# Making the low parts of the MLP weights with accumulating DMAs instead of VectorE

## The chip, the core and the metric

The kernel runs as one program on one core of a Trainium2 chip. The metric is the device time of one execution in microseconds (us), as the median of several runs. Five engines work side by side, each in the order of its own instruction stream: TensorE (PE, with its weight loads shown as PEld), VectorE (DVE), ScalarE (ACT), GpSimd (POOL) and SyncE (SP), which here only issues DMAs. They meet through semaphores.

## The reference, cut to what matters

A backbone of two layers over 512 latent tokens and 256 context tokens, model width 1024. Each layer is an attention mixer followed by an MLP with 4096 hidden units; the part that the change touches is the MLP:

```
def sq_relu_mlp(h, w1, w2):
    return jnp.square(jax.nn.relu(h @ w1)) @ w2

x  = layer_norm(alpha * x + g_m * sq_relu_mlp(x * (1.0 + sc_m) + sh_m, mlp_w1[i], mlp_w2[i]), ...)
if need_ctx:   # only in the first layer: the context tokens go through the same MLP
    xc = layer_norm(alpha * xc + cg_m * sq_relu_mlp(xc * (1.0 + csc_m) + csh_m, mlp_w1[i], mlp_w2[i]), ...)
```

Everything is float32. So the first MLP (layer 0) has 768 tokens, in six tiles of 128, and the second (layer 1) has 512, in four.

## The kernel before

Matrix products are made in a three-term form. A float32 operand x is split into a high part, x rounded to the type fp32r, and a low part, x minus that high part, rounded to fp32r as well. A product is then high times high, high times low and low times high: three matmuls where one would stand.

A weight block is 128 rows of 1024 float32 values, 512 KB. `weight()` (line 72) brings one in: SP issues a DMA from HBM into a `raw` tile (line 69; three buffers, shared with the loads of `w_ada`), ACT writes the high part `wh` as a cast of `raw` (`split_hi`, line 62), and DVE writes the low part `wl` as `raw` minus `wh` (`split_lo`, line 65). There are six buffers of `wh` and six of `wl`. A `raw` buffer is free for the next load when DVE has read it.

`mlp()` (from line 940 on) takes the 4096 hidden units in sixteen chunks c of two blocks each (G = 2). For one chunk, `up(c)` brings in two blocks of `w1` and `up_mm(c)` multiplies them with the activations: TensorE lines 977 (wh with the activations' high part), 980 (wh with their low part) and 981 (wl with their high part), once for each of eight slices k, so the first matmul that reads `wl` is the third of its group. `up_end(c)` makes the hidden tile: ReLU on ACT (line 988), square on DVE (line 989), high part `hh` on ACT (line 62), low part `hl` on DVE (line 65). `w2_of(c)` brings in two blocks of `w2`, and `down(i, ...)` multiplies them for each token tile i with `hh` and `hl`: TensorE lines 89 (high, high), 90 (the one that reads `wl`) and 91. DVE adds the result to `yacc` (line 1059); for the first chunk ACT copies it (line 1057). The loop of a chunk is: `w2_of(c)`, `up(c+1)` with its matmuls, then `down` of chunk c. The last two chunks (R = 2) are multiplied together after the loop. In layer 1, where all tiles have one gate, the `w2` blocks of these last two chunks, four in all, are multiplied by the gate on POOL first (`gate=`, line 75).

In layer 0, steps of other work are put between the tiles of a chunk (`fill`, `ada_vec` from line 177 on): the loads of `w_ada`, weighted sums of them on DVE (line 197), on ACT (line 206) and on POOL (line 208, one pass over a 128x1024 tile).

The order in which each engine takes its instructions is not the order of the program text. The framework simulates the kernel while building it and orders each engine's stream by that simulation. Once built, a stream is fixed: an instruction whose operand is late holds up everything behind it on its engine. So TensorE can take the first matmuls of the next `up` between the tiles of a `down`, where the simulation saw the `down` waiting.

Of the kernel before, what the change touches and what calls it, by code (L numbers as in the profile page):

```python
# [11 lines left out]
F32 = mybir.dt.float32  # L12
F32R = mybir.dt.float32r
AF = mybir.ActivationFunctionType
ALU = mybir.AluOpType
# [4 lines left out]
P = 128  # L20
# [14 lines left out]
G = 2  # L35
# [4 lines left out]
def backbone(ctx, tc, a, out):  # L40
# [3 lines left out]
    nc = tc.nc  # L44
# [16 lines left out]
    def split_hi(dst, src):  # L61
        return nc.scalar.copy(out=dst, in_=src)  # L62

    def split_lo(dst, src, hi):
        return nc.vector.tensor_tensor(out=dst, in0=src, in1=hi.bitcast(F32), op=ALU.subtract)  # L65

    def raw_tile(src, n):
        raw = wpool.tile([P, 1024], F32, name="raw", tag="raw", bufs=3)
        nc.sync.dma_start(raw[:, 0:n], src)
        return raw  # L70

    def weight(src, n=1024, wp=None, tiles=None, gate=None):
        raw = raw_tile(src, n)
        if gate is not None:
            nc.gpsimd.tensor_tensor(out=raw, in0=raw, in1=gate, op=ALU.mult)
        if tiles is not None:
            wh, wl = tiles
        elif wp is None:
            wh = wpool.tile([P, 1024], F32R, name="wh", tag="wh", bufs=6)
            wl = wpool.tile([P, 1024], F32R, name="wl", tag="wl", bufs=6)  # L80
        else:
            wh = wp.tile([P, 1024], F32R, name="wxh", tag="wxh", bufs=2)
            wl = wp.tile([P, 1024], F32R, name="wxl", tag="wxl", bufs=2)
        split_hi(wh[:, 0:n], raw[:, 0:n])
        split_lo(wl[:, 0:n], raw[:, 0:n], wh[:, 0:n])
        return wh, wl

    def mm3(o, lh, ll, rh, rl, start, stop):
# [357 lines left out]
    with tc.manual_schedule(engines={nc.tensor.engine, nc.scalar.engine, nc.vector.engine}):  # L446
        ts = ada_load(0)
        bias00 = [ada_bias(a["b_ada00"][:, i * 256 : i * 256 + 256], 256, nc.scalar) for i in range(2)]
        brows.reverse()
        xs = x_load(0)  # L450
        wraw, wts0 = [], []

        def weight0(k):
            cs = slice((k % 2) * 512, (k % 2) * 512 + 512)
            raw, (wh, wl) = wraw[-1], wts0[-1]
            split_hi(wh[:, cs], raw[:, cs])
            split_lo(wl[:, cs], raw[:, cs], wh[:, cs])

        def weight0_load(i):
            wraw.append(raw_tile(a["w_qkv"][i], 1024))  # L460
            wts0.append([wpool.tile([P, 1024], F32R, name=nm, tag=nm, bufs=6) for nm in ("wh", "wl")])

        weight0_load(0)
        ada_steps(ts)
        ada_row0(0)
        ada_done(0)
        x_act(0, xs, lambda: weight0(0))
        for k in range(KD):
            if k < KD - 1:
                ts = ada_load(k + 1)  # L470
                xs = x_load(k + 1)
                if k % 2 == 1:
                    weight0_load((k + 1) // 2)
                ada_steps(ts)
                ada_row0(k + 1)
                qkv_mm(k, [2], wts0, accs)
                ada_done(k + 1)
                x_act(k + 1, xs, lambda: weight0(k + 1))
                qkv_mm(k, [3, 4, 5, 0, 1], wts0, accs)
            else:  # L480
                qkv_mm(k, [2, 3, 4, 5, 0, 1], wts0, accs)
# [174 lines left out]
    def early_weights(src, ws, n, i0, i1, step, at):  # L656


        def load(k):
            ws.append(raw_tile(src[k], 1024))  # L660

        def split(k):
            raw = ws[k]
            wh, wl = (wpool.tile([P, 1024], F32R, name=nm, tag=nm, bufs=6) for nm in ("wh", "wl"))
            tc.keep_in_program_order(split_hi(wh, raw))
            tc.keep_in_program_order(split_lo(wl, raw, wh))
            ws[k] = wh, wl

        for k in range(n):
            at.setdefault(i0 + step * k, []).append(lambda k=k: load(k))  # L670
            at.setdefault(i1 + step * k, []).append(lambda k=k: split(k))
# [268 lines left out]
    def mlp(layer, tiles, aH, aL, x_src, late, zst, lnst, fill, before_tail, finish):  # L940
# [9 lines left out]

        def up(c):
            if c not in ups:
                ws = [weight(a["mlp_w1"][layer, c * G + j]) for j in range(G)]
                if nt == 6:
                    Hs = [big()[:, :, 0:384] for j in range(G)]
                    parts = [[(H[:, i, :], i * 384, i * 384 + 384) for i in range(2)] for H in Hs]
                else:
                    H = big()
                    Hs = [H[:, j : j + 1, :] for j in range(G)]
                    parts = [[(h[:, 0, i * 256 : i * 256 + 256], i * 256, i * 256 + 256) for i in range(2)] for h in Hs]  # L960
                    if c > 1:
                        parts = [[(h[:, 0, :], 0, 512)] for h in Hs]
                ups[c] = (ws, Hs, parts)
            return ups[c]
# [30 lines left out]
            return out_h  # L995

        def w2_of(c, gate=None):
            return [weight(a["mlp_w2"][layer, c * G + j], gate=gate) for j in range(G)]

        def down(i, hid, w2):  # L1000
            accs = [one(), one()]
# [503 lines left out]
```

## Time and profile before

| | |
|---|---|
| median of 3 runs | 1699.05 us (1697.37 to 1703.05) |
| the profiled execution | 1703.23 us, of which 1701.4 us are the span from the first to the last instruction |
| TensorE busy | 1629.9 us, 96% of the span |
| VectorE busy | 1111.5 us, 65% |
| ScalarE busy | 719.5 us, 42% |
| GpSimd busy | 450.6 us, 26% |
| data moved by DMA | 172.05 MB, mean 101 GB/s |
| mean granted TensorE clock | 0.989 of full speed |

The profile is of one execution. "Busy" is the time in which the engine had an instruction running; matmuls overlap, so a TensorE that is busy without a break has no idle time to win back, and the starts of its matmuls show its pace. All times inside the execution are counted from the span's start. The MLP of layer 0 lies at about 412 to 970 us, that of layer 1 at about 1317 to 1701 us.

### The profile page before, as it was taken

What the parts mean: (1) busy time and instruction counts of PE and PEld (TensorE: products, weight loads), DVE (VectorE), ACT (ScalarE), POOL (GpSimd) and SP (SyncE); (2) the same over time, 40 slices, a digit from 0 to 9 for tenths busy, and PEclk for the clock granted to TensorE, in tenths of its full rate; (3) what the DMA queues carried; (4) which work ended last, traced back from release to release, by engine and by line L of the source; (5) the groups of instructions that cost most, each with busy time, mean ns of one, the idle gap of its engine ahead of it and who ended that gap; (6) DMA issues with size and microseconds to landing.
All of it is one profiled execution on the core that took longest, in us unless ns stands there. A gap on an engine that the chain in (4) does not pass through costs nothing.

```text
span 1701.4 us, 23714 instructions
## 1 busy us (share of the span) xinstructions
PE 1629.9 (96%) x9266; PEld 1369.1 (80%) x9266; DVE 1111.5 (65%) x1700; ACT 719.5 (42%) x1317; POOL 450.6 (26%) x317
## 2 busy tenths in 40 slices
PE   8997998999999999999999899999999999999996
PEld 6775776778888888898889798888778888888884
DVE  4778778755756666556447776766658655555577
ACT  3324666644633344333122356666663532222221
POOL 0247889000323345224003431000004200000034
PEclk9998999999999999999999999999999999999998
DMA  8312113033434356344212232001013533322322
GB/s 323 133 66 90 51 57 100 26 136 112 161 122 138 112 184 198 114 147 146 68 50 85 73 104 90 1 1 38 21 60 122 182 99 99 99 98 88 99 75 75
DMA packets 51969, 172.05 MB, mean 101 GB/s; under 512 B 6776, under 2 KB 6928, under 8 KB 51856
## 3 DMA queue, kind: packets, MB, share of 16 engines
q1 hardware_dynamic: 51824, 170.51, 29.8%
q8 instruction: 73, 1.20, 0.3%
q14 instruction: 40, 0.33, 0.1%
q10 hardware_dynamic: 32, 0.02, 0.0%
HBM read 161.03 MB, written 9.47 MB: 100 GB/s over the span
## 4 chain that ended last, share of the span: by engine, by line
PE 68%; DVE 12%; DMA 7%; POOL 6%; ACT 4%; issue 2%; SPq 0%; DVEq 0%; POOLq 0%; ACTq 0%
PE one L89 9%; PE one L91 9%; PE one L90 9%; PE big L977 7%; PE big L981 6%; PE big L980 6%; DMA araw<-in_w_ada_dram 4%; PE one L731 4%; PE one L917 2%; PE one L921 2%; PE one L918 2%; DVE wl L65 2%; PE one L707 2%; POOL aacc L208 2%; DMA raw<-in_mlp_w_dram 2%
## 5 line engine op out<-in xcount | busy, mean ns | idle before, releaser
L62 ACT CAST wh<-raw 128x1024 fp32r<-128x1024 f32 (+3 forms) x172 | 171.9, 1016 | 399.3 <-PE one L91 213.2
L65 DVE TENSOR_TENSOR wl<-raw,wh 128x1024 fp32r<-128x1024 f32 (+3 forms) x172 | 219.8, 1291 | 173.1 <-ACT wh L62 171.6
L977 PE MATMUL big<-actH,wh 128*128 128x384 f32 (+2 forms) x800 | 280.4, 351 | 1.6 <-ACT wh L62 1.6
L981 PE MATMUL big<-actH,wl 128*128 128x384 f32 (+2 forms) x800 | 279.7, 350 | 0.8 <-DVE wl L65 0.8
L980 PE MATMUL big<-actL,wh 128*128 128x384 f32 (+2 forms) x800 | 279.6, 350 | 0.0
L89 PE MATMUL one<-wh,hh 128*128 128x512 f32 x640 | 256.3, 402 | 12.6 <-ACT hh L62 7.0
L91 PE MATMUL one<-wh,hl 128*128 128x512 f32 x640 | 254.5, 399 | 5.3 <-DVE hl L65 5.3
L90 PE MATMUL one<-wl,hh 128*128 128x512 f32 x640 | 255.5, 399 | 1.3 <-DVE wl L65 1.3
L1059 DVE TENSOR_TENSOR yacc<-yacc,one 128x512 f32<-128x512 f32 x260 | 174.0, 682 | 109.9 <-PE one L91 109.6
L208 POOL TENSOR_TENSOR xr<-xr,raw 128x1024 f32<-128x1024 f32 x49 | 129.7, 2647 | 244.8 <-ACT raw L206 229.6
L977 PEld LDWEIGHTS big<-actH,wh 128*128 128x128 f32 x800 | 150.1, 188 | 15.0 <-ACT wh L62 2.4
L981 PEld LDWEIGHTS big<-actH,wl 128*128 128x128 f32 x800 | 150.1, 188 | 14.1 <-DVE wl L65 1.4
L980 PEld LDWEIGHTS big<-actL,wh 128*128 128x128 f32 x800 | 150.2, 188 | 12.3 <-issue 0.4
L89 PEld LDWEIGHTS one<-wh,hh 128*128 128x128 f32 x640 | 122.0, 191 | 44.5 <-ACT hh L62 8.0
L691 ACT ACTIVATE prob<-big,nm 128x768 f32<-128x768 f32 x128 | 116.2, 908 | 92.2 <-DVE nm L690 91.8
L91 PEld LDWEIGHTS one<-wh,hl 128*128 128x128 f32 x640 | 121.5, 190 | 35.0 <-DVE hl L65 6.2
L90 PEld LDWEIGHTS one<-wl,hh 128*128 128x128 f32 x640 | 122.1, 191 | 27.5 <-DVE wl L65 1.7
L328 POOL TENSOR_TENSOR xr<-xr,ln_g 128x1024 f32<-128x1024 f32 x14 | 37.2, 2658 | 390.9 <-DMA xr<-xres 384.6
L690 DVE TENSOR_REDUCE nm<-big 128x1 f32<-128x768 f32 x128 | 119.8, 954 | 31.8 <-PE big L1360 19.0
L707 PE MATMUL one<-ident,prob 128*128 128x128 f32 x832 | 104.8, 275 | 2.9 <-ACT pT L710 2.0
L731 PE MATMUL one<-pT,V 128*64 128x256 f32 x768 | 98.0, 391 | 5.7 <-DVE pT L712 4.5
L707 PEld LDWEIGHTS one<-ident,prob 128*128 128x128 f32 x832 | 96.0, 142 | 6.8 <-ACT pT L710 2.7
(245 smaller groups left out, 2822.9 us busy)
## 6 DMA issues: line engine op xcount, KB each, us to landing
raw<-in_mlp_w_dram SPq DMA_DIRECT2D x128, 512.0 KB
raw<-in_w_ada_dram SPq DMA_DIRECT2D x56, 512.0 KB
sraw<-in_w_ada_dram SPq DMA_DIRECT2D x16, 512.0 KB
araw<-in_w_ada_dram SPq DMA_DIRECT2D x32, 256.0 KB
raw<-in_w_o_dram SPq DMA_DIRECT2D x16, 512.0 KB
xr<-xres SPq DMA_DIRECT2D x14, 512.0 KB
raw<-in_w_qkv_dram SPq DMA_DIRECT2D x12, 512.0 KB
xres<-z SPq DMA_DIRECT2D x10, 512.0 KB
```

Source lines behind the costliest of these rows:

```text
L62: return nc.scalar.copy(out=dst, in_=src)
L65: return nc.vector.tensor_tensor(out=dst, in0=src, in1=hi.bitcast(F32), op=ALU.subtract)
L89: nc.tensor.matmul(o, lh, rh, start=start, stop=False)
L90: nc.tensor.matmul(o, lh, rl, start=False, stop=False)
L91: nc.tensor.matmul(o, ll, rh, start=False, stop=stop)
L208: nc.gpsimd.tensor_tensor(out=accs[s], in0=accs[s], in1=dst, op=ALU.add)
L707: nc.tensor.transpose(tp[:, j * P : (j + 1) * P], pts[j % 2][:, k * P : (k + 1) * P], ident)
L731: nc.tensor.matmul(acc[64 * hh : 64 * hh + 64, 0:256], v(kts[n], hh), PT[:, :, n, hh, :], start=(n == 0), stop=(n == len(kts) - 1),)
L977: mm = nc.tensor.matmul(o, wh[:, ks], aH[:, k, s:e], start=(k == 0), stop=False)
L980: nc.tensor.matmul(o, wh[:, ks], aL[:, k, s:e], start=False, stop=False)
L981: nc.tensor.matmul(o, wl[:, ks], aH[:, k, s:e], start=False, stop=(k == KD - 1))
L1059: nc.vector.tensor_tensor(out=yacc[i][:, cs], in0=yacc[i][:, cs], in1=accs[hf], op=ALU.add)
```

## The change

A second function, `weight_dma(src)`, makes the two parts of a weight block in another way. The load of `raw` by SP and the cast to `wh` on ACT stay. Then ACT writes `wl` as minus `wh`, and POOL issues a DMA that reads the same 512 KB of the weight from HBM once more and adds them to what `wl` holds. `up()` calls it for all `w1` blocks, `w2_of()` for the `w2` blocks without a gate. The four gated blocks, and all weights outside the two MLPs, go on through `weight()`. The other two edits only write the buffer count of `wh` and `wl` in another form, with the same six.

```
+    def weight_dma(src):
+
+        raw = raw_tile(src, 1024)
+        wh = wpool.tile([P, 1024], F32R, name="wh", tag="wh", bufs=6)
+        wl = wpool.tile([P, 1024], F32R, name="wl", tag="wl", bufs=6)
+        split_hi(wh, raw)
+        nc.scalar.mul(wl, wh.bitcast(F32), -1.0)
+        nc.gpsimd.dma_start(out=wl, in_=src, accum_op=ALU.add)
+        return wh, wl
...
-            wts0.append([wpool.tile([P, 1024], F32R, name=nm, tag=nm, bufs=6) for nm in ("wh", "wl")])
+            wts0.append([wpool.tile([P, 1024], F32R, name=nm, tag=nm, bufs=m) for nm, m in (("wh", 6), ("wl", 6))])
...
-                ws = [weight(a["mlp_w1"][layer, c * G + j]) for j in range(G)]
+                ws = [weight_dma(a["mlp_w1"][layer, c * G + j]) for j in range(G)]
...
-            return [weight(a["mlp_w2"][layer, c * G + j], gate=gate) for j in range(G)]
+            return [weight_dma(a["mlp_w2"][layer, c * G + j]) if gate is None else weight(a["mlp_w2"][layer, c * G + j], gate=gate) for j in range(G)]
```

## Rows read from the trace of the kernel before

**Rows 1.** Page, busy time of each engine over the span.
```profile
PE 1629.9 (96%) x9266; PEld 1369.1 (80%) x9266; DVE 1111.5 (65%) x1700; ACT 719.5 (42%) x1317; POOL 450.6 (26%) x317
```
**Rows 2.** Windows: stretch, length, busy by engine, granted clock, DMA share, GB/s.
```profile
448.00:640.00 192.00, 183.37 (x932) 160.37 (x931) 121.44 (x123) 78.93 (x86) 65.16 (x24) 1.00 0.44 144
939.00:970.00 31.00, 26.18 (x104) 20.28 (x103) 22.24 (x35) 6.35 (x7) 16.21 (x12) 0.89 0.21 65
1343.00:1361.00 18.00, 15.22 (x58) 11.97 (x59) 11.46 (x10) 9.54 (x15) 4.15 (x2) 0.91 0.33 113
1383.50:1405.80 22.30, 22.30 (x97) 17.98 (x96) 12.27 (x16) 6.25 (x9) 0.00 (x0) 1.00 0.29 95
```
**Rows 3.** One window of the same form, inside the `fill` stretch of layer 0.
```profile
505.00:540.00 35.00, 32.13 (x162) 28.75 (x161) 29.01 (x25) 14.46 (x15) 17.46 (x7) 1.00 0.61 194
```
**Rows 4.** What TensorE waited for: total us, times, longest us.
```profile
PE one L91 <- DVE hl L65: 5.3, 2, 2.8
PE one L89 <- DVE yacc L1059: 3.0, 2, 2.8
PE one L90 <- DVE wl L65: 1.3, 1, 1.3
```
**Rows 5.** Instructions by form: busy us, mean ns, idle time before.
```profile
L62 ACT CAST wh<-raw 128x1024 fp32r<-128x1024 f32 x152 | 157.2, 1050 | 393.4 <-PE one L91 213.0 <-PE big L980 133.3 <-DMA raw<-in_mlp_w_dram 38.8
L65 DVE TENSOR_TENSOR wl<-raw,wh 128x1024 fp32r<-128x1024 f32 x152 | 203.0, 1348 | 171.2 <-ACT wh L62 170.8
L266 POOL TENSOR_TENSOR rs<-rs,nhalf 128x1 f32<-128x1 f32 x26 | 15.9, 611 | 177.7 <-DVE rs L263 167.0 <-ACT CKH L62 10.5
```
**Rows 6.** Chain that ended last, in order of time: two loads of `raw`.
```profile
625.98 3.31 DMA raw<-in_mlp_w_dram
...
630.39 2.81 DVE wl L65
...
633.22 5.17 DMA raw<-in_mlp_w_dram
```
**Rows 7.** Timeline of SP: one issue of such a load.
```profile
428.06 0.33 SPq L69 DMA_DIRECT2D raw<-in_mlp_w_dram  x1
```
**Rows 8.** Timeline of ACT in layer 1, one chunk: casts to `wh`.
```profile
1405.31 2.00 ACT L62 CAST wh<-raw 128x1024 fp32r<-128x1024 f32 x2 [8.26 <-PE one L91]
1409.04 1.05 ACT L62 CAST wh<-raw 128x1024 fp32r<-128x1024 f32 x1 [1.73 <-PE big L980]
```
**Rows 9.** Timeline of TensorE, layer 1: two starts of an `up`, one first read of `wl`.
```profile
1375.56 0.39 PE L977 MATMUL big<-actH,wh 128*128 128x512 f32 x1
...
1420.73 0.39 PE L981 MATMUL big<-actH,wl 128*128 128x512 f32 x1
...
1643.80 0.39 PE L977 MATMUL big<-actH,wh 128*128 128x512 f32 x1
```
**Rows 10.** Timeline of ACT in layer 0, one chunk: a cast to `wh`.
```profile
726.98 1.05 ACT L62 CAST wh<-raw 128x1024 fp32r<-128x1024 f32 x1 [5.16 <-PE big L980]
```
**Rows 11.** Timeline of TensorE: the first read of that chunk's `wl`.
```profile
741.38 0.34 PE L981 MATMUL big<-actH,wl 128*128 128x384 f32 x1
```
**Rows 12.** Timeline of ACT where the MLPs begin: first cast to `wh`.
```profile
406.81 1.05 ACT L62 CAST wh<-raw 128x1024 fp32r<-128x1024 f32 x1 [0.63 <-PE one L921]
...
1311.95 1.07 ACT L62 CAST wh<-raw 128x1024 fp32r<-128x1024 f32 x1
```
**Rows 13.** Timeline of TensorE there: first read of `wl`.
```profile
412.96 0.42 PE L981 MATMUL big<-actH,wl 128*128 128x384 f32 x1
...
1317.28 0.37 PE L981 MATMUL big<-actH,wl 128*128 128x256 f32 x1
```
**Rows 14.** Timeline of DVE: subtractions that stand ahead of the hidden tiles.
```profile
939.23 2.18 DVE L65 TENSOR_TENSOR wl<-raw,wh 128x1024 fp32r<-128x1024 f32 x2
...
1333.72 7.90 DVE L65 TENSOR_TENSOR wl<-raw,wh 128x1024 fp32r<-128x1024 f32 x3 [0.17 <-ACT wh L62]
```
**Rows 15.** Timeline of POOL: its longest run without a gap in layer 0.
```profile
465.49 8.89 POOL L208 TENSOR_TENSOR xr<-xr,raw 128x1024 f32<-128x1024 f32 x3 [10.91 <-ACT raw L206]
```

More of the change, by code (lines that the diff above doesn't have):

```diff
@@ L663, in split @@
             raw = ws[k]
-            wh, wl = (wpool.tile([P, 1024], F32R, name=nm, tag=nm, bufs=6) for nm in ("wh", "wl"))
+            wh, wl = (wpool.tile([P, 1024], F32R, name=nm, tag=nm, bufs=m) for nm, m in (("wh", 6), ("wl", 6)))
             tc.keep_in_program_order(split_hi(wh, raw))
```

## The prediction, made before the changed kernel ran

> **What bounds the kernel now.** I read the busy times first [rows 1]: TensorE is busy for 96% of the span, so an edit that takes work from VectorE can only win back TensorE's gaps. The windows show where gaps are [rows 2, 3]. A chunk of layer 1 has none: 22.3 us busy in 22.3 us. In layer 0 the stretch from 448 to 640 us lacks 8.6 us; the ends of layer 0 (939 to 970) and the start of layer 1 (1343 to 1361) lack 4.8 and 2.8 us, with the clock down to 0.89 and 0.91. The list of waits tells who ends the gaps [rows 4]: `wl` itself only 1.3 us in its largest entry, the hidden tiles' low part `hl` 5.3 us, `yacc` 3.0 us. VectorE's subtraction is on time nearly everywhere; what counts is how late its replacement may come.
>
> **What goes and what comes, in engine time.** Of 128 MLP blocks, 124 change (the four gated ones don't). VectorE loses 124 x 1.35 = 167 us, ScalarE gains 124 x 1.05 = 130 us if the negation costs what the cast over the same shape costs [rows 5]. ScalarE has room for it (6.25 us busy in a chunk of 22.3; four negations add 4.2) [rows 2]. Neither sum is time by itself, as neither engine sets a chunk's end.
>
> **The price of one accumulating DMA.** No row shows one, so I bound it. A plain load of the same 512 KB takes 3.31 to 5.17 us in the chain [rows 6]; that is the lower end, 3.3. It has two streams to read, the weight and `wl`; two slow loads one after the other are 10.3 us, the upper end. I take two quick ones, 6.6 us, since the second stream is short of a full HBM load but the pair must meet. As to the DMA engines: four loads fill 0.29 of 22.3 us [rows 2], 1.62 us of all sixteen per load, so a load is 1.6 us of moving and 1.7 us of fixed delay; an accumulate I take as 3.2 us of moving (bounds 1.6 and 4.8). The issue on POOL lies between SP's 0.33 us [rows 7] and a whole POOL pass, 3.0 us [rows 15]; I take the 0.6 us of POOL's smallest tensor operation [rows 5], because issuing touches no tile.
>
> The Trainium skill speaks to this price ("Collectives: The Full Stack", section "The bandwidth ceiling: the fold count and why AG ≠ RS ≠ AR"): an add in the DMA datapath costs nothing itself, but needs two source reads and so runs at half the rate of a copy. No run here shows it yet; by it the sum below would stay as it is. By the plain load's row it would be that of the first rival.
>
> **Chunks of layer 1.** After the end of a `down`, ScalarE casts two blocks from 1405.31 on, those of `w2`, which are needed more than 20 us later. The block that counts is the first `w1` block: its cast starts at 1409.04, when its buffer comes free [rows 8], and TensorE first reads its `wl` at 1420.73 [rows 9], 11.7 us later. Alone, the new chain needs cast 1.05, negation 1.05, issue 0.6, DMA 6.6 = 9.3 us: it fits. But it is not alone. With a negation behind each cast, ScalarE is at this block by 1409.4 and done by 1411.5; its accumulate is issued at 1412. Since 1406.4 three loads (each cast frees a `raw` buffer) and the two `w2` accumulates have been put before the same DMA engines. In order of arrival that is 3 x 1.6 + 3 x 3.2 = 14.4 us of moving from 1406.4, so to 1420.8, and 1.7 us of fixed delay: 1422.5, 1.8 us after the need. TensorE's order is fixed, so everything behind waits. There are 13 such boundaries (starts of `up` from 1375.56 to 1643.80, 22.35 us apart) [rows 9]: +23 us. A single gap of this size should not cost clock as well: the stretch 505 to 540 has 2.9 us of gaps at full clock [rows 3]; those that cost clock were pairs of 2 to 3 us close together.
>
> The skill prices the issue otherwise ("DMA: Bandwidth & Descriptors", Specifications): about 1 us to the first byte from GpSimd, 0.6 us from SyncE. That 0.4 us more at 13 boundaries would add an estimated 5 us; the issue rows here show no such DMA.
>
> **Chunks of layer 0.** Buffer free at 726.98, `wl` read at 741.38 [rows 10, 11]: 14.4 us against 9.3, and the `w2` accumulates were issued 6 us earlier. It hides, by about 5 us. Two things work on it. POOL is in order, and its runs of `fill` passes last up to 8.9 us [rows 15]; an issue caught behind one comes 3.8 us too late. Some seven such runs up to 700 us are longer than 6 us; if a quarter catch a critical issue at half that, it is +3 us. Conversely an issue waits for its negation and holds back the line 208 passes behind it, which free `raw` buffers. Against that, VectorE loses four passes a chunk and `raw` comes free after the cast instead of after a subtraction of up to 2.8 us [rows 6]: of the gaps ended by `wl` and `yacc` I take back 3 us.
>
> **Starts and ends.** Layer 0's first block: cast done at 407.9, plus 1.05 + 0.6 + 6.6 gives 416.1, where TensorE wants it at 412.96 [rows 12, 13]: 3.1 us; ScalarE also has other work between the cast and the negation, so I take +4. Layer 1's: 1313.0 + 8.25 = 1321.3 against 1317.28: +4. What VectorE gives back: three subtractions, 7.9 us, stand ahead of the first hidden tiles until 1341.6; most of that lies beside the ReLU that the tiles need first, so I take back -2; two more, 2.2 us, stand ahead of layer 0's last hidden tile, -2 [rows 14]. The gated blocks at the very end don't change.
>
> **Sum.** 23 + 4 + 4 - 2 - 2 + 3 - 3 = +27 us. The profiled execution, 1703.2, becomes 1730; it was 4.2 us above the median of the runs, so from 1699.05 I predict 1726 us. A difference under 0.3%, 5 us, can't be told from none.
>
> **Rivals.** (a) Faster: the accumulate is as cheap as a load (3.3 us, 1.6 of moving). Then the critical block lands at 1406.4 + 6 x 1.6 + 1.7 = 1417.7, 3 us early, and the 23 go; the starts shrink by 3.3 each to about 1.4 together, POOL's term to nothing, and VectorE's relief remains in full (-4 on the ends, -5 on the gaps by `wl` and `yacc`): 1699 - 7.6 = 1691. It turns at about 2.6 us of moving per accumulate. For it: DMA engines that are idle for 70% of a chunk [rows 2]. Against: two streams. (b) DMA-bound: 4.8 us of moving, 10.3 in all. Then the sum of moving is 3 x 1.6 + 3 x 4.8 = 19.2, landing at 1427.3, 6.6 late, 13 times: +86; the starts +14; and layer 0, whose `fill` stretches already hold the engines at 0.61 [rows 3], gets four times 4.8 us more per 34 us chunk, 0.57, and runs over: some 3 us in each of ten chunks, +30. Less 7 of relief: 1699 + 123 = 1822. (c) The order changes: the simulation that orders TensorE sees the later `wl` and leaves the ten early matmuls of `up` until after the `down`. Then the need moves back by over 5 us, the boundaries cost nothing, and the starts and ends remain: +8 - 4 + 3 - 3 = +4: 1703.
>
> **How the numbers follow.** Forecast 0.45; (a) 0.20, of which 0.12 are over 0.3% faster; (b) 0.20; (c) 0.15, half of it within 0.3% (0.08), 0.03 faster by luck of the order, 0.04 slower. The forecast itself has 0.01 at no change, and 0.44 slower. Faster 0.15, same 0.08 + 0.08 + 0.01 = 0.17, slower 0.44 + 0.20 + 0.04 = 0.68. The range takes in (a) and (c) and the lower half of (b): 1690 to 1800; the forecast's own is 1707 to 1760.
>
> **What would show it.** Right: in layer 1 each `up` begins with a gap of 1 to 3 us ended by a DMA into `wl`, the DMA share rises from 0.29 to about 0.85, and both MLPs start 4 us late. Wrong: no gaps at 22.3 us per chunk (a or c, told apart by the order), or gaps over 5 us with the DMA share near 1 (b). A POOL that spends several us on one issue would also make it wrong: then line 208 sets layer 0.

## The result, and the profile after

The changed kernel takes 1755.05 us (median of four runs, 1751.05 to 1763.72) where the kernel before takes 1699.18 beside it: 1.0333 times as long, with a 95% interval of 1.0289 to 1.0376. It is slower, as forecast, and inside the range, but by 56 us where the sum said 27.

The page of the changed kernel: the busy times (they answer to [rows 1]), the software queue that carries the accumulates (packets, MB, share of the sixteen DMA engines' span), the groups of the new instructions, and the accumulate's median from issue to landing.

```profile
PE 1645.3 (93%) x9266; PEld 1374.9 (78%) x9266; DVE 953.9 (54%) x1576; ACT 837.4 (48%) x1441; POOL 551.0 (31%) x441
...
q0 software_dynamic: 17856, 65.02, 20.1%
...
L95 POOL DMA_DIRECT2D wl<-in_mlp_w_dram x124 | 107.9, 871 | 488.7 <-ACT wl L94 392.7
...
L94 ACT ACTIVATE wl<-wh 128x1024 fp32r<-128x1024 f32 x124 | 127.8, 1053 | 0.7
...
wl<-in_mlp_w_dram POOLq DMA_DIRECT2D x124, 512.0 KB, 8.1
```

The reader is to see two things. First, the prices were guessed well: the negation takes 1.05 us as assumed, the issue 0.87 us (0.6 assumed), and an accumulate holds the sixteen engines for 20.1% of 1761.7 us / 124 = 2.86 us (3.2 assumed). Only from issue to landing it is longer, 8.1 us in the middle, against 6.6. Second, TensorE does the same 9266 matmuls, yet is busy 15.4 us longer: it ran them at a lower granted clock (0.982 of full speed in the mean, against 0.989). The span grew by 60.3 us, so some 45 us are new idle time. The profiled execution of the changed kernel is its slowest, 1763.72 us, so its losses add up to more than the 56 us of the medians.

Where it went is read from windows. I cut both executions at the first matmul of each MLP's `up` and at the first transpose behind layer 0's last chunk. Columns as in [rows 2]; first before, then after; the rows are the MLP of layer 0, the work between, and the MLP of layer 1 to the end.

```profile
412.47:969.67 557.20, 543.56 (x2745) 483.18 (x2744) 349.24 (x377) 195.98 (x213) 174.01 (x72) 0.99 0.38 125
969.67:1316.86 347.19, 341.14 (x2135) 289.27 (x2134) 234.88 (x439) 208.71 (x491) 44.94 (x58) 1.00 0.16 54
1316.86:1701.40 384.54, 365.17 (x1649) 297.95 (x1648) 235.62 (x290) 110.55 (x147) 48.67 (x23) 0.98 0.31 103
```
```profile
409.99:1007.64 597.65, 558.13 (x2746) 491.50 (x2744) 268.12 (x315) 253.81 (x275) 223.91 (x135) 0.97 0.65 172
1007.64:1354.90 347.26, 341.19 (x2136) 289.28 (x2135) 232.41 (x437) 209.72 (x493) 45.56 (x59) 1.00 0.16 55
1354.90:1761.70 406.80, 369.34 (x1649) 298.67 (x1647) 163.12 (x232) 167.73 (x207) 97.22 (x83) 0.97 0.69 174
```

Layer 1 lost 22.3 us (forecast 23 + 4 - 2 = 25), what lies between nothing, layer 0 40.4 us (forecast 4 + 3 - 3 - 2 = 2). So layer 1 came out near the sum, and layer 0 is what has to be explained.

TensorE's timeline in layer 1 of the changed kernel, three of its twelve gaps that a DMA into `wl` ends; they answer to [rows 9, 13]:

```profile
1362.73 0.58 PE L991 MATMUL big<-actH,wl 128*128 128x256 f32 x1 [6.20 <-DMA wl<-in_mlp_w_dram]
...
1493.88 0.71 PE L991 MATMUL big<-actH,wl 128*128 128x512 f32 x1 [2.63 <-DMA wl<-in_mlp_w_dram]
...
1614.14 0.50 PE L991 MATMUL big<-actH,wl 128*128 128x512 f32 x1 [0.46 <-DMA wl<-in_mlp_w_dram]
```

Two gaps belong to the start (6.2 and 3.7 us). The ten others stand at the first read of `wl` in an `up`, at ten of the thirteen boundaries that the prediction counted, 0.46 to 2.63 us, 14.1 us together: the predicted picture. Layer 1's 22.3 us are these 24.0 us of gaps and 4.2 us more of busy TensorE (369.34 against 365.17), less 5.9 us of other gaps that are gone.

In layer 0 TensorE's gaps add up to 39.2 us, against 13.5 before: 19.4 ended by a DMA into `wl` (none before), 7.4 by `yacc` (3.0), 6.6 by `wh` (1.6). The other 14.6 us of the 40 are slower matmuls. The longest gap inside the fill stretch shows how a block of `w1` comes late. First the chain that ended last of the kernel before, then that of the changed one, for the same step (start, length, what):

```profile
471.97 2.42 POOL xr L208
474.41 3.30 DMA raw<-in_mlp_w_dram
477.73 1.06 ACT wh L62
...
480.06 3.61 DMA raw<-in_mlp_w_dram
...
486.03 4.42 DMA raw<-in_mlp_w_dram
490.48 1.05 ACT wh L62
491.55 1.24 DVE wl L65
...
492.83 0.44 PE big L981
```
```profile
469.09 11.14 DMA raw<-in_w_ada_dram
...
480.33 1.80 DVE xr L207
...
482.21 1.17 ACT raw L216
...
483.53 2.37 POOL xr L218
...
501.49 7.10 DMA wl<-in_mlp_w_dram
...
508.63 0.69 PE big L991
```

Before, this path already ends at TensorE: a POOL pass frees `raw`, the `w1` blocks are loaded one after another, and from the last landing (490.45) to the matmul it is cast and subtraction, 2.4 us. Nothing is to spare. After, a load of `w_ada` lands 11.14 us after a buffer came free for it ([rows 6] has 3.3 to 5.2 for loads of the same 512 KB); the two loads issued before it took 6.7 and 8.4 us. POOL had issued four accumulates between 462.00 and 471.87. The passes on the late block end at 485.90, and the same way from landing to matmul takes 9.6 us: cast at 499.05, negation, issue at 501.49, 7.10 us of DMA. TensorE stands 5.0 us.

### The profile page after: what moved, and what is told of

Its sections match the earlier page's. It is cut to its first block, busy times and chain, and to the rows that moved or that the text cites. A ratio compares the mean times of both kernels' runs of the same rounds, so it can differ in the third digit from the quotient of the medians.

```text
span 1761.7 us, 23974 instructions
## 1 busy us (share of the span) xinstructions
PE 1645.3 (93%) x9266; PEld 1374.9 (78%) x9266; DVE 953.9 (54%) x1576; ACT 837.4 (48%) x1441; POOL 551.0 (31%) x441
## 3 DMA queue, kind: packets, MB, share of 16 engines
q0 software_dynamic: 17856, 65.02, 20.1%
## 4 chain that ended last, share of the span: by engine, by line
PE 56%; DMA 16%; DVE 13%; issue 6%; ACT 6%; POOL 3%; DVEq 0%; SPq 0%; POOLq 0%; ACTq 0%
DMA wl<-in_mlp_w_dram 8%; PE one L99 7%; PE one L101 7%; PE one L100 7%; DMA raw<-in_w_ada_dram 6%; PE one L741 5%; PE big L991 4%; PE big L987 4%; PE big L990 4%; PE one L717 2%; DVE nm L700 2%; POOL xr L218 2%; PE one L927 2%; DMA raw<-in_mlp_w_dram 2%; PE one L928 2%
## 5 line engine op out<-in xcount | busy, mean ns | idle before, releaser
L991 PE MATMUL big<-actH,wl 128*128 128x384 f32 (+2 forms) x800 | 283.9, 356 | 38.2 <-DMA wl<-in_mlp_w_dram 38.2
L987 PE MATMUL big<-actH,wh 128*128 128x384 f32 (+2 forms) x800 | 284.3, 356 | 10.1 <-ACT wh L62 6.6
L95 POOL DMA_DIRECT2D wl<-in_mlp_w_dram x124 | 107.9, 871 | 488.7 <-ACT wl L94 392.7
L218 POOL TENSOR_TENSOR xr<-xr,raw 128x1024 f32<-128x1024 f32 x49 | 125.7, 2565 | 126.0 <-ACT raw L216 118.7
L999 DVE TENSOR_TENSOR r<-r 128x768 f32<-128x768 f32 (+1 forms) x64 | 66.6, 1061 | 136.9 <-ACT r L998 136.9
L94 ACT ACTIVATE wl<-wh 128x1024 fp32r<-128x1024 f32 x124 | 127.8, 1053 | 0.7
```

What stands on the lines that cost most here:

```text
L94: nc.scalar.mul(wl, wh.bitcast(F32), -1.0)
L218: nc.gpsimd.tensor_tensor(out=accs[s], in0=accs[s], in1=dst, op=ALU.add)
L987: mm = nc.tensor.matmul(o, wh[:, ks], aH[:, k, s:e], start=(k == 0), stop=False)
L991: nc.tensor.matmul(o, wl[:, ks], aH[:, k, s:e], start=False, stop=(k == KD - 1))
```

## The experiments

Times in us; "layer 0" and "layer 1" are cut out of each profiled execution as above; the whole is the median, with its ratio to the kernel before beside it (1698.1 to 1700.1 us). A layer's time is that of one execution: layer 0 of e1 and e8, where nothing is changed, has 557.8 and 554.4 us, and the profiled execution can lie off the median (the change 1763.7 against 1755.1, e5 1747.0 against 1754.2, the middle of two runs at 1747 and two at 1761, e16 1731.9 against 1737.4).

| | whole | ratio (95%) | layer 0 | layer 1 |
|---|---|---|---|---|
| before | 1699.2 | | 557.2 | 384.5 |
| the change | 1755.1 | 1.0333 (1.0289 to 1.0376) | 597.6 | 406.8 |
| e1_layer1 | 1719.6 | 1.0111 (1.0086 to 1.0135) | 557.8 | 402.5 |
| e2_w2 | 1717.9 | 1.0107 (1.0081 to 1.0133) | 570.3 | 387.4 |
| e3_traffic | 1752.1 | 1.0315 (1.0283 to 1.0348) | 609.7 | 383.9 |
| e4_narrow | 1710.4 | 1.0066 (1.004 to 1.0091) | 567.7 | 381.0 |
| e5_fill_dve | 1754.2 | 1.0326 (1.0277 to 1.0375) | 579.1 | 408.3 |
| e6_before_fill_dve | 1690.2 | 0.9935 (0.9914 to 0.9955) | 546.2 | 381.3 |
| e7_act_copies | 1702.7 | 1.0015 (1.0002 to 1.0027) | 557.3 | 385.2 |
| e8_w2_layer1 | 1699.9 | 0.999 (0.998 to 1.0) | 554.4 | 381.6 |
| e9_pool_copies | 1718.0 | 1.0108 (1.009 to 1.0125) | 575.8 | 384.9 |
| e10_pool_tiny | 1704.2 | 1.0017 (1.0004 to 1.003) | 556.5 | 384.6 |
| e11_traffic_fill_dve | 1713.2 | 1.0079 (1.0054 to 1.0103) | 570.8 | 384.8 |
| e12_fill_dve_w2 | 1689.3 | 0.9934 (0.9922 to 0.9947) | 546.5 | 383.7 |
| e13_plain | 1714.7 | 1.0094 (1.0063 to 1.0125) | 566.5 | 387.2 |
| e14_pool_wh | 1698.9 | 1.0004 (0.9988 to 1.0019) | 560.9 | 381.5 |
| e15_pool_wh1 | 1701.0 | 1.0004 (0.9988 to 1.0019) | 564.1 | 378.1 |
| e16_acc_wh1 | 1737.4 | 1.022 (1.0193 to 1.0247) | 590.0 | 381.8 |
| e17_acc_halves | 1721.4 | 1.0135 (1.0112 to 1.0157) | 581.7 | 382.0 |
| e18_halves | 1753.4 | 1.0317 (1.0294 to 1.0339) | 590.7 | 401.4 |

### Which blocks, and lateness against traffic (e1 to e4)

Against the changed kernel, e1 does it in layer 1 alone, e2 for `w2` alone, e4 accumulates 128 of 1024 columns:

```
e1  -  ws = [weight_dma(a["mlp_w1"][layer, c * G + j]) for j in range(G)]
    +  ws = [(weight_dma if layer == 1 else weight)(a["mlp_w1"][layer, c * G + j]) for j in range(G)]
       (and w2_of with "and layer == 1")
e2  +  ws = [weight(a["mlp_w1"][layer, c * G + j]) for j in range(G)]
e4  -  nc.gpsimd.dma_start(out=wl, in_=src, accum_op=ALU.add)
    +  nc.gpsimd.dma_start(out=wl[:, 0:128], in_=src[:, 0:128], accum_op=ALU.add)
```

> The accumulating DMAs in the MLP of layer 1 alone; layer 0 makes its low parts on VectorE as before. In the trace of the change layer 0 grew by 40 us (557.4 to 597.8, first up to first transpose behind the last chunk) and layer 1 by 22 us (384.5 to 406.8). If the two losses are separate: 1699 + 22 = 1721, plus or minus 4, and the layer 0 of before. If layer 0's loss was a matter of how the whole program was ordered, not of its own DMAs: part of the 40 us stays, 1730 or more.

> Accumulating DMAs for the w2 blocks alone, w1 on VectorE as before. Theory A, lateness: what costs is that w1's chain (negation, issue, landing of 8 us) is longer than the time between a buffer coming free and its first read, and w2 has over 20 us: then nothing is left but noise, 1695 to 1703. Theory B, shared DMA engines: in layer 0 the added moving (2.8 us per accumulate) holds up the loads of raw for fill and weights; half the traffic leaves a third to a half of layer 0's 40 us: 1710 to 1720.

> The change, but each accumulating DMA adds 128 of the 1024 columns only (64 KB instead of 512), so seven eighths of wl stay at minus the high part and the output is not the reference's; negation, issue and waits remain. Theory B (shared DMA engines): most of the loss goes, 1700 to 1708, and so it does by theory A as far as a shorter DMA lands sooner (5 us instead of 8). If POOL's queue or ScalarE's negation is what is late: 1725 or more stays.

In e3 VectorE makes the low parts as before, and POOL accumulates each finished one into a DRAM tile that nobody reads (cut to its main lines; the first write into each of the four tiles is a plain copy):

```
     split_hi(wh, raw)
-    nc.scalar.mul(wl, wh.bitcast(F32), -1.0)
-    nc.gpsimd.dma_start(out=wl, in_=src, accum_op=ALU.add)
+    split_lo(wl, raw, wh)
+    nc.gpsimd.dma_start(out=extra[n], in_=wl.bitcast(F32), accum_op=ALU.add)
```

> The low parts are made on VectorE as before; beside each, once it is made, POOL issues an accumulating DMA of the same 512 KB from it into a spare DRAM tile that nobody reads (124 blocks, both layers), so this adds the moving and the issues but no wait for TensorE. Theory A (lateness of wl): within 4 us of 1699. Theory B (shared DMA engines): the loads of raw slow down, 1710 to 1725, nearly all of it in layer 0. Were POOL's in-order queue the cause, the same, with line 208's passes late rather than the loads long.

The two layers part here. In layer 1 the loss is lateness of `w1` alone: e3, with all the traffic and nothing late, has 383.9 us there; e2, with only `w2` late, 387.4; e1 402.5. In layer 0 it is not: e3 loses 52.5 us there although its low parts come from VectorE. The whole of e1 and e2 fell where one of their theories had it; e3, at 1752.1, is 27 us over the higher of its two ranges, and e4, at 1710.4, just over its lower one. In e4 an eighth of the bytes, holding the engines for 4.0% of the span, still costs layer 0 10.5 us and layer 1 nothing.

### POOL's order, and the DMA engines' time (e5 to e8)

e5 takes the sums of `fill` off POOL in the changed kernel, so that no line 218 pass stands behind an accumulate; e6 is the same edit in the kernel before, as a control. e7 is the kernel before with two plain copies of each finished `wh` of the 124 blocks into spare DRAM, issued by ScalarE. e8 is the kernel before with only the `w2` blocks of layer 1 from chunk 2 on made by accumulates.

```
e5, e6  -  mult = lambda k, s: "dve" if s == 0 and k > 0 else "act"
        +  mult = lambda k, s: "dve" if k > 0 else "act"
           (and mult for every v in fill0)
e7      +  for _ in range(2):  nc.scalar.dma_start(out=extra[n], in_=wh.bitcast(F32))
e8      +  weight_dma(...) if gate is None and layer == 1 and c > 1 else weight(...)
```

> The change, with the fill sums of layer 0 taken off POOL: every step after the first multiplies and adds in one pass on VectorE (line 207), so POOL has no line 218 passes between its accumulating DMAs and raw comes free without POOL. If layer 0's loss (40 us; 52 us with the moving alone) comes from POOL's order, its passes late behind issues that wait: layer 0 falls to 560 to 570 us, total 1722 to 1732. If it is the shared DMA engines that make the loads of raw long: layer 0 stays at 585 to 605, total 1745 to 1765.

> Control for the run above: the kernel before, with the same edit of the fill sums and nothing else. VectorE gets 49 more passes of 1.3 us or more and loses none, so 1699 to 1710; the difference of the two runs is what the accumulating DMAs cost when POOL has nothing else to do.

> The kernel before with moving alone and without POOL: beside each of the 124 blocks, ScalarE issues two plain DMAs of 512 KB from wh to spare DRAM tiles that nobody reads, about the moving of one accumulate (2 x 1.5 us of the sixteen engines), with low parts on VectorE as before. Shared DMA engines: layer 0 at 590 to 615 us, as with the accumulates into DRAM (609.7), layer 1 near 385 to 390, total 1735 to 1760. POOL's order: layer 0 within 5 us of 557, total 1699 to 1706.

> Accumulating DMAs only where the experiments found neither lateness nor a crowd: w2 in layer 1 from chunk 2 on (24 blocks), everything else as before. Lateness and sharing both predict no loss, 1695 to 1701; a gain of some 2 us if VectorE's relief is worth anything there. Over 1706 would say that something else costs time in layer 1.

e5 lies 32.9 us above its control in layer 0 and 27.0 in layer 1, so with no POOL pass of the fill left to hold back, four fifths of layer 0's loss are still there. (Its layer 0, 579.1 us, lies between the two ranges written down; its whole, 1754.2, in the higher one.) And e7 holds the engines for another 20.2% of the span, as long as the accumulates do, at a ratio of 1.0015; that is where its expectation had put "POOL's order", and e10 below speaks against that reading. So neither POOL's passes nor the engines' time alone explain layer 0. e8 shows an accumulate that costs nothing: needed late, no other loads in a hurry. e6, meant as a control and expected at 1699 or more, is 0.65% faster than the kernel before.

### The same order of instructions, one thing changed (e9 to e16)

The build orders each engine's stream by a simulation, so an edit can reorder everything. Three pairs have the same streams, instruction by instruction, on every engine: e3 and e9; the change and e13; e15 and e16. In each pair the only difference is whether the DMA adds or merely copies (an add's issue also holds POOL longer, 0.87 us against 0.54). The other kernels have orders of their own: TensorE's matmuls stand otherwise in 380 of 9266 places between e9 and e10, in 728 between e14 and e16.

```
e9   e3 with       +  nc.gpsimd.dma_start(out=extra[n], in_=wl.bitcast(F32))
e10  e9 with 16 columns: out=extra[n] of [P, 16], in_=wl[:, 0:16]
e11  e3 with the edit of e6
e13  the change with  +  nc.gpsimd.dma_start(out=wl, in_=src)
e14  e7 with       +  nc.gpsimd.dma_start(...)  in place of nc.scalar
e15  e14 with one copy per block
e16  e15 with      +  accum_op=ALU.add
```

> The low parts stay on VectorE as before; for each of the 124 MLP blocks POOL also issues a plain copy of the finished wl (512 KB) into a spare DRAM tile that nobody reads. It is e3_traffic without the adding, so with about half its moving (some 1.5 us of the sixteen engines per copy instead of 2.9). Theory P (POOL is in order: an issue that waits for VectorE's wl holds back the line 218 passes that free raw, the raw loads of w1 come late, and with them casts, low parts and yacc behind them): the copies wait as e3's did, so layer 0 stays 35 to 55 us longer than before's 557 us, the whole at 1735 to 1755 us. Theory M (the accumulating kind of DMA, or its second stream, slows the loads of raw): with no accumulate and half the moving, layer 0 falls back to 557 to 570 us, the whole at 1700 to 1713 us.

> As e9_pool_copies, but each copy takes only 16 of 1024 columns of wl, so next to nothing is moved; POOL's wait for wl and its issue (some 0.9 us) stay. Theory P (POOL's order): layer 0 is 30 to 55 us longer than before all the same, the whole at 1730 to 1755 us. Theory M (accumulates or their moving slow the loads): as before, 1697 to 1706 us. Layer 1, whose fill runs nothing on POOL, stays at 381 to 386 us by both.

> e3_traffic (low parts on VectorE, POOL accumulates each finished wl into a spare DRAM tile) with the sums of the fill on VectorE, so that no line 218 pass stands on POOL behind an accumulate. Its control is e6_before_fill_dve: layer 0 546 us, whole 1690. Theory P (the harm goes through the passes behind the accumulates on POOL): layer 0 falls from e3's 610 us to 546 to 556, the whole at 1688 to 1702 us. Theory M (accumulates slow the raw loads whatever stands on POOL): layer 0 stays 20 us or more above 546, the whole over 1710 us.

> The change as it is, in the same order of instructions on every engine, but the DMA into wl only overwrites it with the weights and adds nothing (so the low parts are not the reference's): one stream to read instead of two. By the copies of e9_pool_copies its moving is some 1.3 us instead of 2.9, its landing some 6 us instead of 8. If the second stream is what costs (in layer 0 by slowing the loads of raw, in layer 1 by landing late), layer 0 falls from 598 to 565 to 578 us and layer 1 from 407 to 382 to 392, the whole to 1708 to 1725 us. If the harm is the order of instructions, the waits on POOL or the negations on ScalarE, all of which stay, layer 0 stays at 590 us or more and the whole over 1735 us.

> e7_act_copies (low parts on VectorE, two plain copies of the finished wh into spare DRAM per block, which cost nothing: layer 0 at 557 us) with the same two copies issued by POOL instead of ScalarE, so through the software queue. If it is the software queue that harms the loads beside it, layer 0 is 590 us or more (its moving is as much as that of e3_traffic, 610 us) and the whole over 1735 us. If moving of itself is harmless when its data are ready early and the order is e7's, layer 0 stays below 565 us and the whole at 1700 to 1710 us.

> As e14_pool_wh with one copy per block instead of two, so with the moving of e9_pool_copies (layer 0 at 576 us), but of wh, which is ready earlier than wl. If the software queue's moving costs in proportion, layer 0 is 570 to 580 us, the whole at 1712 to 1722; if e9's loss came from the lateness of wl on POOL or from its order, 555 to 562 us and the whole at 1698 to 1706.

> e15_pool_wh1 (low parts on VectorE, one copy of each finished wh into spare DRAM, issued by POOL; no change in time) with the copies made accumulating ones, in the same order of instructions on every engine. The sixteen engines are then held for some 20% of the span, as in e14_pool_wh (19.5%), which cost nothing. If an accumulate slows what runs beside it more than a copy that holds the engines as long, layer 0 goes from 564 to 585 us or more and the whole to 1720 us or more. If only the time that the engines are held counts, or lateness of what is waited for, as in e14: layer 0 under 570 us, the whole at 1698 to 1706 us.

e10 speaks to POOL's order. Its waits are long: in layer 0 of the change POOL waited 186 us for ScalarE's negations; what POOL waited for in layer 0 of e10 (total, times, longest), and the window of its layer 0:

```profile
POOL extra L99 <- DVE wl L65: 229.4, 62, 18.5
```
```profile
414.61:971.16 556.55, 545.26 (x2745) 485.13 (x2744) 352.81 (x377) 196.05 (x213) 207.44 (x134) 0.99 0.38 126
```

229 us of waiting and 62 more issues in line, and layer 0 has its 557 us: POOL's waits by themselves cost nothing. e11 comes from the other side: with no `fill` pass behind its accumulates it still loses 24.6 us of layer 0 to its control e6. That is less than half of e3's 52.5, so passes that stand behind accumulates may carry a part; e5 and e11 have other orders than the kernels they are compared with, so how much is not shown.

The three pairs then show what the adding costs: layer 0 gets 33.9 us longer from e9 to e3, 31.2 from e13 to the change, 25.9 from e15 to e16. In layer 1 it is 19.6 us from e13 to the change; where no low part waits for it, 3.7 from e15 to e16 and -1.0 from e9 to e3. e13, with windows of both layers and its landing time, the counterpart to the rows of the changed kernel above:

```profile
410.97:977.46 566.49, 545.41 (x2745) 484.26 (x2744) 268.75 (x315) 254.04 (x275) 205.78 (x135) 0.99 0.55 182
1324.69:1711.90 387.21, 366.05 (x1649) 298.63 (x1647) 167.35 (x232) 167.98 (x207) 76.71 (x83) 0.97 0.54 183
```
```profile
wl<-in_mlp_w_dram POOLq DMA_DIRECT2D x124, 512.0 KB, 5.2
```

With one stream to read the DMA lands in 5.2 us instead of 8.1 and holds the engines 11.6% of 1711.9 us / 124 = 1.60 us instead of 2.86. TensorE's gaps behind a DMA into `wl` in layer 0 shrink from 19.4 to 5.3 us, and its busy time falls back from 558.1 to 545.4.

What the adding does to the loads beside it is seen in e15 and e16, where VectorE makes the low parts in time. VectorE's timeline, three passes on blocks of `w_ada` in the fill stretch, e15 first:

```profile
463.89 1.28 DVE L212 SCALAR_TENSOR_TENSOR xr<-raw,scT,xr 128x1024 f32<-128x1024 f32 x1 [0.38 <-DMA raw<-in_w_ada_dram]
466.43 1.29 DVE L212 SCALAR_TENSOR_TENSOR xr<-raw,scT,xr 128x1024 f32<-128x1024 f32 x1 [1.26 <-DMA raw<-in_w_ada_dram]
468.90 2.17 DVE L212 SCALAR_TENSOR_TENSOR xr<-raw,scT,xr 128x1024 f32<-128x1024 f32 x1 [1.18 <-DMA raw<-in_w_ada_dram]
```
```profile
464.94 1.28 DVE L215 SCALAR_TENSOR_TENSOR xr<-raw,scT,xr 128x1024 f32<-128x1024 f32 x1 [0.38 <-DMA raw<-in_w_ada_dram]
469.33 1.83 DVE L215 SCALAR_TENSOR_TENSOR xr<-raw,scT,xr 128x1024 f32<-128x1024 f32 x1 [3.11 <-DMA raw<-in_w_ada_dram]
472.49 1.29 DVE L215 SCALAR_TENSOR_TENSOR xr<-raw,scT,xr 128x1024 f32<-128x1024 f32 x1 [1.32 <-DMA raw<-in_w_ada_dram]
```

Layer 0 begins 1.26 us later in e16 (410.77 against 409.51). Counted from there, the first pass starts 0.2 us earlier than in e15, the second 1.6 us later and the third 2.3, and the second pass waits 3.11 us for its load where e15's waits 1.26. VectorE takes its work in order, so `yacc` comes late behind them: what ended waits in layer 0 of e16 (total, times, longest), and the same of e15:

```profile
PE one L107 <- DVE yacc L1077: 26.2, 11, 8.2
DVE xr L215 <- DMA raw<-in_w_ada_dram: 20.9, 10, 7.2
```
```profile
DVE xr L212 <- DMA raw<-in_w_ada_dram: 12.9, 8, 5.0
PE one L104 <- DVE yacc L1074: 10.8, 5, 6.3
```

Is it the adding, or the time for which the engines are held? The software queue's line of e14 and of e16:

```profile
q0 software_dynamic: 35712, 130.04, 19.5%
```
```profile
q0 software_dynamic: 17856, 65.02, 19.8%
```

The same share of the engines, in e14 with plain copies of twice the bytes; e14 costs nothing, e16 36 us more than e15. So it is not the software queue, and not the share alone. But it is not that an accumulate slows the loads more, either. The trace's semaphores tell when every load landed; here are the 62 loads of `w_ada` in layer 0:

| run | beside each MLP block | mean us from issue to landing | layer 0 |
|---|---|---|---|
| before | nothing | 3.9 | 557.2 |
| e10 | a copy of 16 columns | 4.0 | 556.5 |
| e15 | a copy of `wh` | 5.0 | 564.1 |
| e9 | a copy of `wl` | 5.2 | 575.8 |
| e7 | two copies, by ScalarE | 5.8 | 557.3 |
| e14 | two copies, by POOL | 6.3 | 560.9 |
| e16 | an accumulate of `wh` | 6.3 | 590.0 |
| e3 | an accumulate of `wl` | 6.6 | 609.7 |

Beside e14's copies the loads land as late as beside e16's accumulates. ScalarE and VectorE wait for loads about as long too, 133 us in layer 0 of e14 and 140 in e16 (96 in e15), but less of it reaches TensorE: its waits for `yacc` are 5.7 us in e14, against 26.2 in e16 above. What ended waits in layer 0, e14 first:

```profile
ACT wh L62 <- DMA raw<-in_mlp_w_dram: 81.1, 29, 8.1
PE one L104 <- DVE yacc L1074: 5.7, 2, 5.3
```
```profile
ACT wh L62 <- DMA raw<-in_mlp_w_dram: 66.0, 24, 6.8
```

So the adding holds the engines for longer, loads beside it land later (5.0 to 6.3 us from e15 to e16, 5.2 to 6.6 from e9 to e3, 4.7 to 5.9 from e13 to the change), and in the order of those kernels that costs 26 to 34 us. In e14's order the same lateness costs nothing, and in e7's nearly the same. In all three pairs the order came out the same with and without the add, so the simulation that sets it seems not to count the longer transfer; for the two copies of e7 and e14 it came out another. That such an order hides the late loads would fit, but no run put e16's accumulates into e14's order.

e9, at 1718.0 us, lies between its two ranges. It fits in there: its plain copies of `wl` cost 18 us, e15's equally large copies of `wh` nothing, though the loads land after 5.2 and 5.0 us. They differ in the order of instructions and in when the source is ready; which of the two it is was not tried.

### Packets, and the best version (e12, e17, e18)

```
e17  e16 with      +  for s in (slice(0, 512), slice(512, 1024)):
                   +      nc.gpsimd.dma_start(out=extra[n][:, s], in_=wh[:, s].bitcast(F32), accum_op=ALU.add)
e18  the change with the same split of its accumulate
e12  e6 and e8 together
```

> As e16_acc_wh1, each accumulate split into two of 512 columns, so with packets of 2 KB in place of 4 KB (and one more issue on POOL per block, which e14_pool_wh had as well). If an accumulate harms because each of its packets holds an engine so long (0.32 us against 0.15 of a load's or a copy's, worked out from the queues' shares) while a load's next packet waits its turn, half as long packets take away half of the harm: halfway between e16 and 1700 us. If the harm is of the accumulate whatever its packets, as e16 or slower.

> The change with each accumulate split into two of 512 columns: packets of 2 KB, two issues of 0.9 us on POOL per block. If the long packets of the accumulates are what slows the loads of raw in layer 0, as e17 against e16 speaks for, layer 0 falls from 598 us to 578 to 588; layer 1 is late by its own chain, and the second issue and the 10% more engine time that e17's halves took leave it at 400 to 410; the whole 1735 to 1748 us. If packets don't matter, layer 0 stays at 595 or more and the whole at 1753 us or more.

> The best of both: the kernel before with the fill's sums on VectorE (1690 us alone) and only the w2 blocks of layer 1 from its third chunk on made by accumulating DMAs, which alone changed nothing (ratio 0.999). If accumulates that are needed late and stand before no POOL work are free and VectorE in layer 1 has room, 1688 to 1692 us: a ratio of 0.993 to 0.996, no better than the fill alone. If VectorE's relief in layer 1 were worth something, under 1687 us.

By the queues' shares one packet of e16 holds an engine for 0.198 x 16 x 1729.9 / 17856 = 0.31 us, one of e14 for 0.15 us, though both carry 4 KB. A load that takes turns with an accumulate on an engine would then wait twice as long for each turn. That is an argument; the loads beside e14's short packets land as late as those beside e16's. With packets of half the size, e17 loses 22.5 us where e16 loses 38.5, near the half that this asks for. But its order of instructions is another one than e16's, and in the changed kernel itself the split gained nothing: e18, 1753.4 us, against the 1735 to 1748 that I had written down. In layer 0 e18 has 590.7 us, between its two ranges. So packet length is not shown to be the reason.

The Trainium skill ("DMA: Bandwidth & Descriptors", section "Queues, rings and completion order") has each DMA engine take turns between the queues that have work for it, one packet at a time, a packet there being several descriptors. By it a load shares its engines with whatever another queue has put there, and the later landings agree (3.9 us before, 6.3 in e14 and e16). It does not settle the length of packets: from e16 to e17 the loss went from 38.5 to 22.5 us, from the change to e18 hardly at all.

e12 beats both kernels, 1689.3 us, but e6 alone has 1690.2: the accumulates add nothing to it. The gain comes with the edit of `fill`. SP's waits for a free `raw` buffer behind the POOL passes, 149.3 us in layer 0 of the kernel before, become 85.0 us behind VectorE's passes in e6 (and 23.9 behind other loads of `w_ada`), and layer 0 is 11 us shorter.

## Why the prediction was right in direction and less than half in size

**The price of an accumulate** held: 0.87 us of issue, 2.86 us of moving, within the bounds; landing at 8.1 us lay in the upper half of 3.3 to 10.3, 1.5 us over the 6.6 of the sum. The Trainium skill's rule ("Collectives: The Full Stack", section "The bandwidth ceiling: the fold count and why AG ≠ RS ≠ AR"), given there for a ring's ReduceScatter, that the add reads two sources and so runs at half a copy's rate, agrees with the runs: 2.86 us against e13's 1.60, 1.8 times.

**Layer 1** held in place and cause; that its size did (22.3 us for 25) is in part luck. The gaps stand at the starts of `up`, ended by `wl`; 10 of 13 boundaries show one of 1.4 us in the mean, where I had 13 of 1.8; the start costs 9.9 us of gaps where I had 4. The boundaries gave 14.1 us for 23; with the measured 2.86 us of moving the prediction's own working gives 0.75 us a boundary, some 10 in all. Against that stand the start and 4.2 us of slower matmuls, which the sum had at nothing. e3 and e13 show the cause: with no low part to wait for, or a DMA that lands 3 us sooner, the layer takes 384 and 387 us.

**Chunks of layer 0** is the step that failed: "It hides, by about 5 us." The terms of layer 0 came to 2 us, and it lost 40.4, 31 of them by the adding (e13 to the change). I took the room from one block, cast at 726.98 and read at 741.38 [rows 10, 11], which lies behind the dense part of the fill. In the fill stretch the chain before has no room: 2.4 us from landing to matmul, all of it cast and subtraction. [rows 4] showed 1.3 us of waiting for `wl`, and I read that as room; it was a path that only just arrived. The new path from landing to matmul is 7 us longer there (9.6 us).

And I asked only when `wl` lands, not what its DMA does to the loads beside it. Rival (b) had that idea, with layer 0 running over, but tied it to 4.8 us of moving. It happened at 2.86: e16 costs layer 0 some 26 us more than e15 though TensorE waits for none of its accumulates. The three buffers of `raw` were the place to start from: in layer 0 of the kernel before SP waits 107 times for a subtraction or a POOL pass to free one (for 121 loads), so a slower load delays those that follow. e14 shows that this is not the whole of it: with loads as late, in another order, it loses nothing.

**POOL**: +3 us for issues caught behind `fill` passes and passes held back by issues. e10 shows that such waits cost nothing while little is moved. Whether passes behind real accumulates cost more than 3 us stays open (e11).

**Relief of VectorE**, -3 us in layer 0's gaps: not seen. Gaps ended by `yacc` rose from 3.0 to 7.4 us, though VectorE does less.

**The clock**: "A single gap of this size should not cost clock as well", and those that did "were pairs". The kernel before itself says otherwise: the gap in [rows 2]'s third line is a single one of 2.78 us at 1345.1, and from 1347.8 to 1351.2 the granted clock is 0.50, while the gap of 2.81 us at 527.7 cost none. In layer 0 of the changed kernel the lower clock made 14.6 us of slower matmuls. Windows behind its gaps of 4.9 us that ended at 416.5 and of 4.5 us that ended at 601.5; the kernel before has a granted clock of 1.00 in both stretches:

```profile
412.00:448.00 36.00, 28.59 (x126) 25.53 (x127) 11.00 (x18) 19.92 (x26) 6.41 (x6) 0.81 0.69 173
576.00:608.00 32.00, 25.81 (x116) 19.51 (x115) 14.60 (x21) 15.52 (x15) 11.90 (x7) 0.87 0.50 137
```

The first window holds two drops to 0.50, from 415.4 to 422.2 and from 439.3 to 446.1. Most of layer 0's gaps that cost clock were longer than those I had sized (5 us, not 1.8). In layer 1's chunks the sentence held at nine of ten gaps: behind the one of 2.63 us that ended at 1493.9 the clock is 0.50 until 1497.4, behind the one of 2.61 us that ended at 1686.9 it stays at 1.00.

What stays open: why loads that land equally late cost e16 36 us more than e15 and e14 nothing; their orders of instructions differ, and no run holds one of them fixed. How much of the 31 us that the adding costs the change in layer 0 is its own late landing and how much the slower loads can't be split exactly either, as every kernel that separates them has another order of instructions.

## What to carry to other kernels

Before a short engine step is replaced by a DMA, look for the stretch in which the step's result is only just in time, not for a typical one: a wait of near nothing in the list of waits can be a path without any room, and the chain of that stretch tells which. Cost the new transfer twice, once for its own arrival and once for what it does to the loads that run beside it, and where loads go through few buffers take the second seriously. Compare variants in the same order of instructions, as the three pairs here are: loads equally late cost 36 us in one kernel and nothing in another that is ordered otherwise. And use an accumulating DMA for what is needed late and has no hurried loads beside it (e8: no change); here the work that VectorE was freed of was hardly what the kernel waited for.

## What the runs showed of the hardware that I had not expected

Plain loads beside accumulates land later, and beside plain copies that hold the engines as long they land just as late: 6.3 us beside 19.8% of the span in accumulates (e16) and beside 19.5% in copies through the same queue (e14), 5.8 us beside 20.2% through ScalarE's queue (e7), 3.9 us in the kernel before. What that lateness cost was 36 us against e15 in e16, and nothing in e14 or e7.

POOL can wait 229 us and issue 62 DMAs more in front of its passes at a ratio of 1.0017 (e10), so what it held back there was not on TensorE's path.

TensorE fell to the lower clock level after single gaps of about 5 us: behind the one at 416.5 its matmuls of 384 columns started 0.32 us apart, against 0.18 at full clock, and the stretch from 415.4 to 422.2 had a granted clock of 0.50. Among gaps of 2.6 to 2.8 us some cost clock (1345.1 before, 1491.2 after) and some did not (527.7 before, 1684.3 after).
